# Making the sums of two of four chunk pairs for channel mixers 2 to 4 in the stage before each mixer

## The chip, the cores and the metric

The kernel runs on one core of one Trainium2 chip. Its engines work side by side, each on its own queue of instructions, in the order in which that queue was written: TensorE (PE in the profile: matmuls; PEld is its weight load), VectorE (DVE), ScalarE (ACT), GpSimd (POOL), and SyncE (SP), which here only issues DMAs. An instruction that waits holds up everything behind it on its engine. The metric is the device time of one execution in microseconds (us), the median of several runs.

## The reference

One sequence of 512 tokens of 1024 features goes through two layers. Each layer is a channel mixer, a token mixer and a second channel mixer, so there are four channel mixers; the token mixers are latent attention (MLA) in layer 1 and sparse attention (NSA) in layer 2.

```python
def rmsnorm(x, g):
    return x * rsqrt(mean(x * x, axis=-1) + 1e-6) * g

def swiglu(x, w_gate, w_up, w_down):          # 1024 -> 2816 -> 1024
    return (silu(x @ w_gate) * (x @ w_up)) @ w_down

for i in range(2):
    h = h + 0.5 * swiglu(rmsnorm(h, ffn_norm_a[i]), ...a[i])
    h = h + mixer_i(rmsnorm(h, mix_norm[i]))  # i = 0: MLA, i = 1: NSA
    h = h + 0.5 * swiglu(rmsnorm(h, ffn_norm_b[i]), ...b[i])
out = rmsnorm(h, final_norm)
```

Everything is float32.

## The kernel before

**Layout.** The residual `h` lies in SBUF transposed: eight chunks `h[0]` to `h[7]`, each 128 features by 512 tokens. A float32 operand is split into a high part (an ACT copy that rounds) and a low part (DVE: the value less the high part), and a product is three matmuls: high weight by high value, high weight by low value, low weight by high value. A chunk's weights can therefore not be multiplied through before DVE has made their low part, which the third matmul reads. Weights arrive by DMA in a raw tile (`wr`, two buffers) and are split into one of two tiles `w` that take turns (`slab_ahead`: ACT L176 the high part, DVE L178 the low part). A `w` tile is free for the next weights when the chunk two places earlier has been multiplied.

**A channel mixer** (`ffn`, called for 0 to 3; I call them mixers 1 to 4) has 22 blocks of 128 hidden units. The first three (`PLAIN`) are done by plain matmuls of `x = h * gain` (`plain`, L401 to L403); call their weight slabs g0, u0, g1, u1, g2, u2 in their order. Blocks 3 to 21 use a form of Strassen's scheme with seven products in place of eight (`wsums`, `product`): it pairs chunk p with chunk p + 4 (p = 0 to 3) and halves of the tokens, and needs for each pair four sums of quarters. `combine(p)` makes them: ACT scales both chunks into `y` (L267, twice), DVE forms four sums of quarters in `u` in three instructions (L271, 128x512; L272 and L273, 128x256 each), and `split` makes high and low part of `u` in a tile `four` (ACT L205 and DVE L206, 128x1024 each). In mixers 2 to 4 the four `combine` calls stand behind the plain blocks: pair 0 behind the first, pair 1 behind the second, pairs 2 and 3 behind the third. `four` has four buffers.

**The end of the stage ahead of a mixer** is where the residual's chunks end, one by one, in the order 0, 4, 1, 5, 2, 6, 3, 7 (`self.order`). Mixer 3 follows mixer 2: there each chunk takes 24 matmuls (L462 to L464) with its own 512-column weights. Mixers 2 and 4 follow attention: there each chunk takes 12 matmuls of 512 columns (`w_o1`, L197 to L199), and one 1024-column weight slab serves two chunks. When a chunk's matmuls end, DVE adds it to the residual (L468, in attention L708), and `norm_chunk` makes `x` of it (ACT L208, DVE L209) and its squares (ACT L285), which POOL sums up (L289).

**What sets the order.** The kernel is written against a layer that records all instructions with their dependences and then schedules each engine's queue by itself; what is written earlier goes first among what is ready in that layer's own reckoning. So a call that is moved in the source moves instructions on ACT and DVE past others, and the result is a fixed queue.

In the built program the chunks are named by a number: `h_101` is chunk 0, `h_102` chunk 1, and so on to `h_108`, chunk 7. The functions that the change touches, with the line numbers of the profile:

Of the kernel before, what the change touches and what calls it, by code (L numbers as in the profile page):

```python
# [11 lines left out]
F32 = mybir.dt.float32  # L12
# [6 lines left out]
P = 128  # L19
# [24 lines left out]
TURN = "mm", "S", "T", "mm", "S", "T", "T"  # L44
FGAINS = "a0", "b0", "a1", "b1"
LASTK = 4
HS = S // 2
KP = KC // 2
PLAIN = 3
PAD = 16  # L50
# [11 lines left out]
class Kern:  # L62
# [157 lines left out]
    def norm_chunk(self, c):  # L220
# [5 lines left out]
        else:  # L226
            self.sumsq(self.h[c], self.s2 is None)

    def norm_split(self, c):
        t = self.xp.tile([P, 2 * S], F32R, tag="x", bufs=KC, name="x")  # L230
        if self.to_ffn:

            g = self.ngains[:, self.nng + c : self.nng + c + 1]
            v = t.rearrange("p (e z n) -> p e z n", e=2, z=2)
            hi, lo, src = v[:, :, 0, :], v[:, :, 1, :], self.h[c].rearrange("p (e n) -> p e n", e=2)
            self.split(src, hi, lo, gain=g)
            for e in range(2):
                self.xc["LR"[e], c] = v[:, e, 0, :], v[:, e, 1, :]
        else:
            self.split(self.h[c], t[:, :S], t[:, S:], gain=self.gains[:, self.ng + c : self.ng + c + 1])  # L240
            self.xh.append(t[:, :S])
            self.xl.append(t[:, S:])
# [12 lines left out]
            return self.xp.tile([P, S], F32R, tag="w2", bufs=2, name="q")  # L255
        return self.qt[(self.nq - self.nq // 3 - 1) % 4]

    def combine(self, p):


        nc, fp = self.nc, self.fp
        y = fp.tile([P, 1024], F32, tag="fh", bufs=3, name="y")
        u = fp.tile([P, 1024 + 2 * PAD], F32, tag="fl", bufs=3, name="u")[:, :1024]
        for e in range(2):
            c = p + KP * e
            with self.tc.issue_after(self.weights.ins) if self.weights else nullcontext():
                nc.scalar.activation(y[:, e * S : e * S + S], self.h[c], AF.Copy, scale=self.gains[:, self.ng + c : self.ng + c + 1])  # L267
            self.weights = None
        q = lambda t, i: t[:, i * HS : i * HS + HS]
        two = lambda t: t.rearrange("p (a n) -> p a n", n=HS)  # L270
        nc.vector.tensor_tensor(two(u[:, :S]), q(y, 1)[:, None, :].to_broadcast([P, 2, HS]), two(y)[:, 0:4:3, :], op=ALU.subtract)  # L271
        nc.vector.tensor_tensor(q(u, 2), q(y, 0), q(u, 1), op=ALU.subtract)  # L272
        nc.vector.tensor_tensor(q(u, 3), q(y, 2), q(u, 2), op=ALU.subtract)  # L273
        t = self.four()
        self.split(u, t[:, :1024], t[:, 1024:])
        for i, j in enumerate((5, 7, 6, 4)):
            self.xc[j, p] = q(t, i), q(t, i + 4)
        for j, x in zip((1, 2, 3), (("L", p), ("L", p + KP), ("R", p + KP))):
            self.xc[j, p] = self.xc[x]
# [116 lines left out]
    def plain1(self, w, k, out):  # L396
        (wh, wl), mm = w, self.nc.tensor.matmul
        for e in range(2):
            (xh, xl), o = self.xc["LR"[e], k], out[:, e * HS : e * HS + HS]

# [26 lines left out]
    def ffn(self, idx, gain_next, ap, tp):  # L427
# [6 lines left out]
        def gate(f, g):  # L434

            t = tg[f] = tp.tile([P, S], F32, tag="tg", bufs=2, name="tg")
            nc.vector.tensor_tensor(t, g, row, op=ALU.mult)
            nc.scalar.activation(t, t, AF.Silu, scale=-1.0)
            nc.vector.tensor_tensor(t, t, row, op=ALU.mult)
# [17 lines left out]
        def down(p, w, b0, b1):  # L457
            for k in range(b0, b1):
                wh, wl = w[0][:, k - b0], w[1][:, k - b0]
                for x in range(0, S, HS):  # L460
                    o, xh, xl = p[:, x : x + HS], ah[k][:, x : x + HS], al[k][:, x : x + HS]
                    nc.tensor.matmul(o, wh, xh, start=k == b0 and x == 0, stop=False, skip_group_check=True)  # L462
# [20 lines left out]
        def tokens(t):  # L483

            xts.append(tp.tile([P, D], F32, tag="fr", bufs=3, name="xt"))
            with self.tc.issue_after(self.high.ins):
                nc.sync.dma_start(xts[t], a["x_tok"][t * P : (t + 1) * P, :])

        def squares(t):
            nc.scalar.activation(xts[t], xts[t], AF.Square, accum_out=sums[:, t : t + 1])  # L490

        def late():
            for c in self.late:
                self.sumsq(self.h[c])
            return self.norm_col(D, self.s2)
# [3 lines left out]
        for f, g in enumerate(gates):  # L499
            u = tu[f] = self.bank(("mm", "S")[f % 2], "pu")  # L500
            if idx == f == 0:
                self.first_block((g, u))
                self.third_slab(a["w_gu"][0, 1, 0])
                self.ahead.insert(0, self.wslab(a["w_gu"][0, 1, 1], (KC, P), "half"))
                for t in range(3):
                    tokens(t)
                squares(0)
                tokens(3)
                squares(1)
            else:  # L510
                self.plain(idx, f, 0, g)
            if f == 0 and idx > 1:
                col = late()
            if f == 1 and idx == 0:
                squares(2)
                squares(3)
                col = self.rsqrt_col(sums, D)
            if idx or f:
                self.plain(idx, f, 1, u)
            if f == 0 and idx == 1:  # L520

                col = late()
            if f == 1:
                nc.scalar.activation(self.tiny[:, 4:5], col[:, 0:1], AF.Silu, scale=-1.0)
                pb = self.norm_bcast(col)
                row = tp.tile([P, S], F32, tag="row", bufs=1, name="row")
                self.spread = nc.scalar.activation(row, pb, AF.Copy)
                for e in range(2):
                    gate(e, gates[e])
                    act(e)  # L530
            elif f:
                gate(f, g)
                act(f)
            for p in (((0,), (1,), (2, 3)) if idx else ((0, 1), (2,), (3,)))[f]:
                self.combine(p)
        t = self.tiny
        for i, g in enumerate(gates[::-1]):
# [32 lines left out]
        if gain_next == "fin":  # L570

            hs, out = [self.parts(self.four(F32)) for _ in range(4)], []
            for t in range(4):
                for b in range(2):
                    p = self.mm_bank("ph")
# [9 lines left out]
        for c in self.order:  # L585
            p = self.mm_bank("pd")
            down(p, self.wslab(a["w_down"][idx, c, :, tail * P :], (NF - tail, P), "act"), tail, NF)
            add(c, p)
            self.norm_chunk(c)
            if ahead and c == self.order[-1]:  # L590
                self.ahead.append(ahead())

    def last(self, src, ah, al, ap, ht, hs):
# [16 lines left out]

        ks = range(NF - LASTK, NF)
        ends = {k: slab(k) for k in ks}
# [91 lines left out]
    def w_o1(self, w, oh, ol, c, e, final):  # L704
        p = self.mm_bank("po")
        for k in range(4):
            self.mm3(p, w[0][:, e, k], w[1][:, e, k], oh[k], ol[k], k == 0, k == 3)
        self.nc.vector.tensor_tensor(self.h[c], p, self.h[c], op=ALU.add)  # L708
        if final:
            self.norm_chunk(c)  # L710

    def stats(self, n):

# [820 lines left out]
```

## Time and profile before

| | |
|---|---|
| Median of 3 runs | 1863.41 us (1863.02 to 1865.26) |
| The profiled execution | 1862.05 us |
| its span, first to last instruction | 1860.3 us |
| PE busy | 1845.7 us, 99% of the span, 14464 matmuls |
| DVE busy | 1507.4 us, 81% |
| ACT busy | 1064.5 us, 57% |
| POOL busy | 296.7 us, 16% |
| granted TensorE clock, mean | 0.999 |

The span is what the profiler saw between the program's first and last instruction; the execution's own time is longer by 1.75 us around it. A matmul is counted as busy from its start to its modelled end, and matmuls overlap, so that a PE wait of less than about 0.17 us does not show as idle time. In the chain of work that ended last, PE has 93% of the span.

### The profile page before, as it was taken

The numbers are of one execution on the slowest core, as the hardware profiler recorded it, in microseconds if no ns is written. First come the engines' busy times: TensorE is split into PE (matmuls) and PEld (weight loads), VectorE is DVE, ScalarE is ACT, GpSimd is POOL, SyncE is SP. The second block draws the span as 40 slices with busy tenths as digits, with TensorE's granted clock in tenths as the row PEclk, the third lists the DMA queues.
The fourth block names the chain that finished last, engine by engine and source line by source line (L and its number), as shares of the span: only waits on it lengthen the run. The fifth ranks groups of instructions, "written<-read, shape, count | busy, mean of one in ns | idle before, by whom it ended". The sixth has DMA issues, their size and how long they took to land.

```text
span 1860.3 us, 37031 instructions
## 1 busy us (share of the span) xinstructions
PE 1845.7 (99%) x14464; PEld 1763.4 (95%) x14464; DVE 1507.4 (81%) x2810; ACT 1064.5 (57%) x1997; POOL 296.7 (16%) x370
## 2 busy tenths in 40 slices
PE   9999999999999999999999999999999999999998
PEld 9999999888889999999999999988888889999997
DVE  8988886688779988886898888666878888888885
ACT  7555553567666555554655545446776865555554
POOL 0000000258830000001000000022666620000000
PEclk9999999999999999999999999999999999999999
DMA  6433331434433433322443332162433133433321
GB/s 238 132 108 103 103 92 48 117 105 103 114 123 112 119 103 109 110 73 72 138 118 110 109 106 81 45 183 82 108 108 103 40 118 116 121 104 107 103 78 69
DMA packets 84351, 196.64 MB, mean 106 GB/s; under 512 B 10944, under 2 KB 38464, under 8 KB 84176
## 3 DMA queue, kind: packets, MB, share of 16 engines
q1 hardware_dynamic: 81664, 191.34, 34.9%
q10 hardware_dynamic: 2512, 2.93, 0.5%
q8 instruction: 114, 1.87, 0.4%
q14 instruction: 61, 0.50, 0.1%
HBM read 178.44 MB, written 2.16 MB: 97 GB/s over the span
## 4 chain that ended last, share of the span: by engine, by line
PE 93%; DVE 3%; ACT 1%; issue 1%; POOL 1%; DMA 0%; ACTq 0%; POOLq 0%; DVEq 0%
PE pd L462 8%; PE pd L464 8%; PE pd L463 8%; PE px L386 6%; PE px L388 6%; PE px L387 5%; PE pg L386 4%; PE pg L388 4%; PE pg L387 4%; PE pq L386 4%; PE pq L388 4%; PE pq L387 4%; PE o L1337 2%; PE pt L1310 2%; PE po L197 2%; PE po L199 2%
## 5 line engine op out<-in xcount | busy, mean ns | idle before, releaser
L462 PE MATMUL pd<-ah,wd 128*128 128x256 f32 x1152 | 318.3, 276 | 0.0
L464 PE MATMUL pd<-ah,wd 128*128 128x256 f32 x1152 | 318.3, 276 | 0.0
L463 PE MATMUL pd<-al,wd 128*128 128x256 f32 x1152 | 318.3, 276 | 0.0
L289 POOL TENSOR_TENSOR s<-s,sq 128x512 f32<-128x512 f32 x38 | 54.7, 1441 | 1050.3 <-ACT sq L285 1050.3
L462 PEld LDWEIGHTS pd<-ah,wd 128*128 128x128 f32 x1152 | 216.3, 188 | 0.0
L464 PEld LDWEIGHTS pd<-ah,wd 128*128 128x128 f32 x1152 | 216.3, 188 | 0.0
L463 PEld LDWEIGHTS pd<-al,wd 128*128 128x128 f32 x1152 | 216.3, 188 | 0.0
L206 DVE TENSOR_TENSOR w<-wr,w 128x1024 fp32r<-128x1024 f32 x72 | 88.2, 1225 | 120.7 <-ACT w L205 120.4
L386 PE MATMUL px<-four,wh 128*128 128x256 f32 x608 | 168.4, 277 | 0.4 <-ACT wh L205 0.2
L388 PE MATMUL px<-four,wl 128*128 128x256 f32 x608 | 168.2, 277 | 0.2 <-DVE wl L206 0.2
L386 PE MATMUL pq<-four,wh 128*128 128x256 f32 x608 | 168.1, 276 | 0.2 <-ACT uq L556 0.2
L387 PE MATMUL px<-four,wh 128*128 128x256 f32 x608 | 168.0, 276 | 0.0
L388 PE MATMUL pq<-four,wl 128*128 128x256 f32 x608 | 167.9, 276 | 0.0
L387 PE MATMUL pq<-four,wh 128*128 128x256 f32 x608 | 167.9, 276 | 0.0
L468 DVE SCALAR_TENSOR_TENSOR h<-pd,h 128x512 f32<-128x512 f32 x216 | 148.3, 686 | 15.4 <-PE pd L464 15.2
L205 ACT ACTIVATE wd<-wdr 128x384 fp32r<-128x384 f32 x192 | 99.2, 519 | 103.8 <-issue 64.6
L176 ACT ACTIVATE w<-wr 128x1024 fp32r<-128x1024 f32 (+3 forms) x89 | 80.8, 908 | 87.5 <-PE pd L464 20.6
L206 DVE TENSOR_TENSOR wd<-wdr,wd 128x384 fp32r<-128x384 f32 x192 | 105.8, 553 | 20.1 <-ACT wd L205 20.0
L178 DVE TENSOR_TENSOR w<-wr,w 128x1024 fp32r<-128x1024 f32 (+3 forms) x75 | 78.3, 1044 | 50.0 <-ACT w L176 49.8
L728 ACT ACTIVATE p<-p,small 128x512 f32<-128x512 f32 (+2 forms) x192 | 106.9, 558 | 19.0 <-DVE small L727 15.3
L386 PEld LDWEIGHTS px<-four,wh 128*128 128x128 f32 x608 | 114.1, 188 | 1.0 <-ACT wh L205 0.4
L388 PEld LDWEIGHTS px<-four,wl 128*128 128x128 f32 x608 | 114.2, 188 | 0.6 <-DVE wl L206 0.6
(379 smaller groups left out, 6264.9 us busy)
## 6 DMA issues: line engine op xcount, KB each, us to landing
wr<-in_w_gu SPq DMA_DIRECT2D x93, 512.0 KB, 3.5
ru<-in_w_gu SPq DMA_DIRECT2D x76, 512.0 KB, 4.3
wdr<-in_w_down SPq DMA_DIRECT2D x192, 192.0 KB, 2.5
wr<-in_w_down SPq DMA_DIRECT2D x24, 256.0 KB, 2.6
wr<-in_mla_w_o SPq DMA_DIRECT2D x8, 512.0 KB, 3.4
th<-btab_d SPq DMA_DIRECT2D x16, 256.0 KB, 3.7
wr<-in_nsa_w_q SPq DMA_DIRECT2D x8, 512.0 KB, 3.8
wr<-in_nsa_w_o SPq DMA_DIRECT2D x8, 512.0 KB, 3.7
```

Source lines behind the costliest of these rows:

```text
L176: self.copied = nc.scalar.activation(wh[:, m], raw[:, m], AF.Copy)
L178: nc.vector.tensor_tensor(wl[:, m], raw[:, m], f32v(wh[:, m]), op=ALU.subtract)
L205: nc.scalar.activation(hi, src, AF.Copy)
L206: (nc.gpsimd if pool else nc.vector).tensor_tensor(lo, src, f32v(hi), op=ALU.subtract)
L386: mm(out, wh[:, p], xh, start=first and p == 0, stop=False, skip_group_check=True)
L387: mm(out, wh[:, p], xl, start=False, stop=False, skip_group_check=True)
L388: mm(out, wl[:, p], xh, start=False, stop=last and p == KP - 1, skip_group_check=True)
L462: nc.tensor.matmul(o, wh, xh, start=k == b0 and x == 0, stop=False, skip_group_check=True)
L463: nc.tensor.matmul(o, wh, xl, start=False, stop=False, skip_group_check=True)
L464: last = nc.tensor.matmul(o, wl, xh, start=False, stop=k == b1 - 1, skip_group_check=True)
L468: nc.vector.scalar_tensor_tensor(self.h[c], p, 0.5, self.h[c], op0=ALU.mult, op1=ALU.add)
L728: nc.scalar.activation(p_sb[:, :n], p_sb[:, :n], AF.Exp, bias=nm, scale=-1.0, accum_out=sm)
```

## The change

`combine` for pairs 0 and 1 (`EARLY`) is called in the stage before mixers 2, 3 and 4, right behind `norm_chunk` of chunk 4 and of chunk 5, the second chunk of each pair. It is not done ahead of mixer 1, whose input comes by DMA. Its scratch (`y` and `u`, 2048 columns in all) is then a buffer of `four` (`spare`), which both early pairs share, since the usual scratch belongs to the mixer's own pools. In the mixer, pair 2 is made behind the first plain block and pair 3 behind the second. The number of instructions of each kind stays as it was.

```diff
+EARLY = 0, 1
...
+    def combine_early(self, c):
+        if self.to_ffn and c - KP in EARLY:
+            if c == KP:
+                self.spare = self.four(F32)
+            self.combine(c - KP, self.spare)
...
-    def combine(self, p):
+    def combine(self, p, spare=None):
...
-        y = fp.tile([P, 1024], F32, tag="fh", bufs=3, name="y")
-        u = fp.tile([P, 1024 + 2 * PAD], F32, tag="fl", bufs=3, name="u")[:, :1024]
+        if spare is None:
+            y = fp.tile([P, 1024], F32, tag="fh", bufs=3, name="y")
+            u = fp.tile([P, 1024 + 2 * PAD], F32, tag="fl", bufs=3, name="u")[:, :1024]
+        else:
+            y, u = spare[:, :1024], spare[:, 1024:]
...
-            for p in (((0,), (1,), (2, 3)) if idx else ((0, 1), (2,), (3,)))[f]:
+            for p in (((2,), (3,), ()) if idx else ((0, 1), (2,), (3,)))[f]:
                 self.combine(p)
...
             add(c, p)
             self.norm_chunk(c)
+            self.combine_early(c)
...
         if final:
             self.norm_chunk(c)
+            self.combine_early(c)
```

In the changed file the lines behind the edits are numbered higher: L178 is L179 there, L206 is L207, L209 is L210, L267 is L277, L271 to L273 are L281 to L283, L285 is L295, L468 is L478, and L708 is L719.

**VectorE, end of mixer 2.** Before, the queue holds for each chunk its addition, the low part of the weights of the chunk two places later, and the low part of `x`. Row 1250 (`w<-wr,w`) makes the low part for chunk 6.

```order
1246 L468 SCALAR_TENSOR_TENSOR h_102<-pd,h_102 128x512
1247 L178 TENSOR_TENSOR w<-wr,w 128x512
1248 L209 SCALAR_TENSOR_TENSOR x<-h_102,ngains,x 128x2x256
1249 L468 SCALAR_TENSOR_TENSOR h_106<-pd,h_106 128x512
1250 L178 TENSOR_TENSOR w<-wr,w 128x512
1251 L209 SCALAR_TENSOR_TENSOR x<-h_106,ngains,x 128x2x256
1252 L468 SCALAR_TENSOR_TENSOR h_103<-pd,h_103 128x512
```

Now the same place reads as follows. `four<-four` at L281 to L283 and L207 are the early pairs: the first pair in rows 1245 to 1252, the second from row 1254.

```order
1246 L478 SCALAR_TENSOR_TENSOR h_102<-pd,h_102 128x512
1247 L282 TENSOR_TENSOR four<-four 128x256
1248 L179 TENSOR_TENSOR w<-wr,w 128x512
1249 L283 TENSOR_TENSOR four<-four 128x256
1250 L210 SCALAR_TENSOR_TENSOR x<-h_102,ngains,x 128x2x256
1251 L478 SCALAR_TENSOR_TENSOR h_106<-pd,h_106 128x512
1252 L207 TENSOR_TENSOR four<-four 128x1024
1253 L210 SCALAR_TENSOR_TENSOR x<-h_106,ngains,x 128x2x256
1254 L281 TENSOR_TENSOR four<-four 128x512
1255 L478 SCALAR_TENSOR_TENSOR h_103<-pd,h_103 128x512
1256 L282 TENSOR_TENSOR four<-four 128x256
1257 L179 TENSOR_TENSOR w<-wr,w 128x512
```

The low part of chunk 6's weights has moved from ahead of chunk 2's addition (`h_103`) to behind it, and behind two instructions of the second pair.

**ScalarE, the same place.** Before, each chunk's weights (`w<-wr`) come ahead of `x` and the squares; row 787 is chunk 6's high part.

```order
784 L176 ACTIVATE w<-wr 128x512
785 L208 ACTIVATE x<-h_102,ngains 128x2x256
786 L285 ACTIVATE sq<-h_102 128x512
787 L176 ACTIVATE w<-wr 128x512
788 L208 ACTIVATE x<-h_106,ngains 128x2x256
789 L285 ACTIVATE sq<-h_106 128x512
790 L176 ACTIVATE w<-wr 128x512
```

Now (row 786 is still chunk 2's high part; `four<-h` at L277 is the scaling, `four<-four` at L206 the high part of the sums):

```order
786 L177 ACTIVATE w<-wr 128x512
787 L209 ACTIVATE x<-h_102,ngains 128x2x256
788 L295 ACTIVATE sq<-h_102 128x512
789 L277 ACTIVATE four<-h_102,gains 128x512
790 L206 ACTIVATE four<-four 128x1024
791 L209 ACTIVATE x<-h_106,ngains 128x2x256
792 L295 ACTIVATE sq<-h_106 128x512
793 L277 ACTIVATE four<-h_106,gains 128x512
794 L177 ACTIVATE w<-wr 128x512 x2
```

The high part of chunk 6's weights now stands behind the first pair's high part, which waits for DVE, and behind all of chunk 5's work.

**VectorE, end of NSA (ahead of mixer 4).** Before, row 2287 (`w<-wr,w`) is the low part of slab g0, the first that mixer 4 multiplies:

```order
2283 L708 TENSOR_TENSOR h_103<-po,h_103 128x512
2284 L178 TENSOR_TENSOR w<-wr,w 128x1024
2285 L209 SCALAR_TENSOR_TENSOR x<-h_103,ngains,x 128x2x256
2286 L708 TENSOR_TENSOR h_107<-po,h_107 128x512
2287 L178 TENSOR_TENSOR w<-wr,w 128x1024
2288 L209 SCALAR_TENSOR_TENSOR x<-h_107,ngains,x 128x2x256
2289 L708 TENSOR_TENSOR h_104<-po,h_104 128x512
```

Now slab g0's low part is row 2297:

```order
2286 L719 TENSOR_TENSOR h_103<-po,h_103 128x512
2287 L179 TENSOR_TENSOR w<-wr,w 128x1024
2288 L207 TENSOR_TENSOR four<-four 128x1024
2289 L210 SCALAR_TENSOR_TENSOR x<-h_103,ngains,x 128x2x256
2290 L281 TENSOR_TENSOR four<-four 128x512
2291 L719 TENSOR_TENSOR h_107<-po,h_107 128x512
2292 L282 TENSOR_TENSOR four<-four 128x256
2293 L719 TENSOR_TENSOR h_104<-po,h_104 128x512
2294 L283 TENSOR_TENSOR four<-four 128x256
2295 L210 SCALAR_TENSOR_TENSOR x<-h_107,ngains,x 128x2x256
2296 L210 SCALAR_TENSOR_TENSOR x<-h_104,ngains,x 128x2x256
2297 L179 TENSOR_TENSOR w<-wr,w 128x1024
```

It has moved behind chunk 3's addition (`h_104`), which needs the end of chunk 3's matmuls, and behind the `x` of chunks 6 and 3.

## Rows read from the trace of the kernel before

**Rows 1.** The page's busy time, share and instructions of the engines.

```profile
PE 1845.7 (99%) x14464; PEld 1763.4 (95%) x14464; DVE 1507.4 (81%) x2810; ACT 1064.5 (57%) x1997; POOL 296.7 (16%) x370
```

**Rows 2.** Busy us by engine, summed over the first 60 us of mixers 2, 3, 4.

```profile
sum 180.00, PE 179.04 PEld 177.49 DVE 162.45 ACT 117.70 POOL 7.98; mean PE 59.68 PEld 59.16 DVE 54.15 ACT 39.23 POOL 2.66
```

**Rows 3.** Timeline of DVE, end of mixer 2: start, us, instruction, idle before.

```profile
870.49 0.69 DVE L468 SCALAR_TENSOR_TENSOR h<-pd,h 128x512 f32<-128x512 f32 x1 [0.48 <-PE pd L464]
871.16 0.69 DVE L178 TENSOR_TENSOR w<-wr,w 128x512 fp32r<-128x512 f32 x1
871.98 0.75 DVE L209 SCALAR_TENSOR_TENSOR x<-h,ngains,x 128x512 fp32r<-128x512 f32 x1
873.22 0.69 DVE L468 SCALAR_TENSOR_TENSOR h<-pd,h 128x512 f32<-128x512 f32 x1 [0.49 <-PE pd L464]
```

**Rows 4.** Timeline of PE there: the third matmul of chunk 6.

```profile
873.24 0.28 PE L464 MATMUL pd<-ah,w 128*128 128x256 f32 x1
```

**Rows 5.** Timeline of ACT, end of mixer 2.

```profile
867.82 0.64 ACT L176 ACTIVATE w<-wr 128x512 fp32r<-128x512 f32 x1 [0.80 <-PE pd L464]
868.50 0.73 ACT L208 ACTIVATE x<-h,ngains 128x512 fp32r<-128x512 f32 x1
869.13 0.62 ACT L285 ACTIVATE sq<-h 128x512 f32<-128x512 f32 x1
```

**Rows 6.** Groups of DVE and ACT: count | busy us, mean ns | idle before.

```profile
L206 DVE TENSOR_TENSOR four<-u,four 128x1024 fp32r<-128x1024 f32 x16 | 19.5, 1222 | 1.5 <-ACT four L205 1.5
L271 DVE TENSOR_TENSOR u<-y 128x512 f32<-128x512 f32 x16 | 10.9, 685 | 0.0
L273 DVE TENSOR_TENSOR u<-y,u 128x256 f32<-128x256 f32 x16 | 6.7, 422 | 0.1
L267 ACT ACTIVATE y<-h,gains 128x512 f32<-128x512 f32 x32 | 20.8, 708 | 0.0
L205 ACT ACTIVATE four<-u 128x1024 fp32r<-128x1024 f32 x16 | 16.8, 1057 | 7.8 <-DVE u L273 7.8
```

**Rows 7.** Timeline of DVE, end of NSA.

```profile
1507.51 1.78 DVE L209 SCALAR_TENSOR_TENSOR x<-h,ngains,x 128x512 fp32r<-128x512 f32 x1
1509.82 1.21 DVE L178 TENSOR_TENSOR w<-wr,w 128x1024 fp32r<-128x1024 f32 x1
1510.95 0.74 DVE L209 SCALAR_TENSOR_TENSOR x<-h,ngains,x 128x512 fp32r<-128x512 f32 x1
1511.61 0.68 DVE L708 TENSOR_TENSOR h<-po,h 128x512 f32<-128x512 f32 x1
```

**Rows 8.** Timeline of POOL, the same place.

```profile
1507.37 1.38 POOL L289 TENSOR_TENSOR s<-s,sq 128x512 f32<-128x512 f32 x1 [0.86 <-ACT sq L285]
```

**Rows 9.** Busy us by engine, 1497 to 1511 us, the end of NSA.

```profile
1497.00:1511.00 14.00, 14.00 (x62) 11.39 (x61) 12.94 (x15) 10.04 (x15) 5.86 (x4) 1.00 0.25 77
```

**Rows 10.** Timeline of PE: mixer 4's third matmul, of slab g0.

```profile
1513.42 0.28 PE L403 MATMUL pg<-x,w 128*128 128x256 f32 x1
```

**Rows 11.** Timeline of DVE, end of MLA: low part of chunks 3 and 7's weights.

```profile
536.22 1.22 DVE L178 TENSOR_TENSOR w<-wr,w 128x1024 fp32r<-128x1024 f32 x1 [0.45 <-ACT w L176]
```

**Rows 12.** Timeline of PE: third matmul of MLA's chunk 3.

```profile
540.77 0.39 PE L199 MATMUL po<-oh,w 128*128 128x512 f32 x1
```

**Rows 13.** Timeline of DVE: slab u2's low part in mixers 2 and 4.

```profile
569.93 1.23 DVE L178 TENSOR_TENSOR w<-wr,w 128x1024 fp32r<-128x1024 f32 x1 [1.28 <-ACT w L176]
...
1537.58 1.23 DVE L178 TENSOR_TENSOR w<-wr,w 128x1024 fp32r<-128x1024 f32 x1 [2.05 <-ACT w L176]
```

**Rows 14.** Page: DMA issues of a chunk's weights, KB, us to landing.

```profile
wr<-in_w_down SPq DMA_DIRECT2D x24, 256.0 KB, 2.6
```

**Rows 15.** Busy us by engine at the end; PEclk ahead of the last two numbers.

```profile
1853.50:1856.20 2.70, 0.00 (x0) 0.00 (x0) 1.91 (x7) 1.46 (x4) 0.00 (x0) 1.00 0.00 0
1856.20:1860.30 4.10, 0.00 (x0) 0.00 (x0) 0.10 (x1) 0.07 (x1) 0.00 (x0) 0.51 0.33 128
```

**Rows 16.** Timeline of PE at the start: ten matmuls of 512 columns.

```profile
1.05 4.63 PE L95 MATMUL warm<-ones 128*128 128x512 f32 x10 [1.05 <-DVE ones L92]
```

## Prediction

> **What bounds the kernel now.** I read the page first: PE is busy for 1845.7 us [rows 1] of a span of 1860.3. So the change, which adds no matmul and takes none away, can only act through PE's waits, in two places: the first tens of us of mixers 2 to 4, from which two of four `combine` calls leave, and the ends of the stages ahead, into which they go. The table by stage gives the first place: in the first 60 us of the three mixers together, PE idles for 180 - 179.04 = 0.96 us [rows 2]. A wait under 0.17 us does not show there, so I allow as much again: about 2 us is all that relief at the mixers' starts can give back.
>
> For the second place I read the timelines. At the end of mixer 2 PE does not idle. The additions of two chunks are 873.22 - 870.49 = 2.73 us apart [rows 3], which is PE's own time for a chunk. DVE keeps that pace because three instructions of 0.69, 0.69 and 0.75 us fit into it, with some 0.5 us of idle time left. What PE waits for next is a weight's low part: chunk 6's is done at 871.16 + 0.69 = 871.85 [rows 3], and chunk 6's third matmul reads it at 873.24 [rows 4], 1.4 us later. So the slack is 1.4 us, and what is put ahead of that instruction decides.
>
> **What a pair costs.** On DVE one instruction of 685 ns, two of 422 (the second shape, L272, is like L273) and one of 1222: 2.75 us. On ACT two of 708 and one of 1057 ns: 2.47 us [rows 6]. In each of three stages two pairs are moved, so 5.5 us of DVE and 4.9 us of ACT; nothing is added over the whole kernel. Instructions that follow each other start some 0.08 us ahead of the listed end of the one before (1509.82 + 1.21 against 1510.95 [rows 7]); I take that off. `combine` issues no DMA.
>
> **End of mixer 2.** The new order puts the low part of chunk 6's weights behind chunk 2's addition. That addition cannot start before chunk 2's matmuls end, 873.22 [rows 3]. Behind it come a 128x256 sum and the low part: 873.22 + 0.69 + 0.42 + 0.69 - 0.16 = 874.9. PE wants it at 873.24, so it waits 1.6 us whatever else happens. That is the lower bound.
>
> DVE will not be ready at 873.22, though, since the sums hang on ACT. Chunk 4's ACT work stands one period ahead of the rows shown for chunk 1: its squares start at 869.13 - 2.73 = 866.4 [rows 5], its scaling ends at 867.7. Then, each step behind the one before:
> - DVE: first sum of pair 0 to 868.4, chunk 1's addition to 869.0.
> - ACT: chunk 1's x, squares and scaling (0.73 + 0.62 + 0.71) to 870.9, pair 0's high part to 871.9, chunk 5's three to 873.8.
> - DVE: first sum of pair 1 to 874.5, chunk 2's addition to 875.1, second sum to 875.4, chunk 6's low part to 876.1.
>
> That is 2.9 us later than PE wants it. POOL makes it worse. In NSA's end an x low part took 1.78 us in place of 0.74 while POOL summed squares at 1507.37 for 1.38 us [rows 7, 8]: it stood until POOL had ended, 1.04 us. Two such sums fall into the walk above, for 2.9 + 2.0 = 4.9 us. At mixer 2's end they now fall into gaps of DVE, and the early pairs fill those gaps. I take the middle, **3.9 us**, bounds 1.6 and 4.9.
>
> The Trainium skill (SBUF — State Buffer, section "Who interferes with whom") says that a VectorE instruction with two SBUF inputs and a GpSimd instruction that reads SBUF lock each other out for a whole instruction, and that the order of issue decides who waits. The trace agrees (the 1.78 us). By that rule alone the term would be 4.9, without it 2.9.
>
> **End of NSA.** Slab g0's low part ended at 1509.82 + 1.21 = 1511.03 [rows 7] and is read at 1513.42 [rows 10]. Now there stand ahead of it: pair 0 (2.75 - 0.3), three sums of pair 1 (1.53 - 0.24), and, which followed it before, x of chunk 6, chunk 3's addition and its x (0.66 + 0.60 + 0.66). Together 5.7 us. DVE idled for 14 - 12.94 = 1.06 us in the 14 us up to then [rows 9]; if all of that is used up, g0's low part ends at 1515.7, 2.2 us late. From below: chunk 3's matmuls end one chunk before g0's first; 12 matmuls of 512 columns are as many columns as 24 of 256, so 2.73 us, at about 1510.5. Addition, one sum, two x and the low part behind it (0.68 + 0.42 + 1.48 + 1.21 - 0.32) end at 1514.0: 0.5 us late. From above: two more collisions with POOL, 4.2. The collisions of before are in the 1511.03 already; I take **2.8 us**. Chunk 7's x now stands behind three scalings on ACT (2.1 us later), but it is read last of g0, which itself starts 2.8 us later; without that cover it would cost up to 2.1 in place of the 2.8.
>
> **End of MLA.** The low part for chunks 3 and 7 ended at 536.22 + 1.22 = 537.44 [rows 11] and is read at 540.77 [rows 12]: 3.3 us of slack. Ahead of it come pair 0 (2.45), chunk 2's addition and chunk 5's x (1.3), less the 0.45 us that DVE idled before it: 540.7, just in time. One or two collisions would make 1 to 2 us. Bounds 0 and 2.0; I take **0.3**.
>
> **The mixers' starts.** DVE gets rid of 5.5 us in the first 15 us. But by slab u2 DVE had caught up even before: it idled 1.28 us in mixer 2 and 2.05 us in mixer 4, waiting for ACT [rows 13]. What comes after that does not know of the early pairs. Bounds 0 and 2.0 us of gain; I take **0.4**.
>
> **Costed at nothing.** The scratch tile needs a `four` buffer whose readers are matmuls of the stage ahead; PE runs in order, so they are over when chunk 0 is multiplied. If they were not, the first scaling would wait and every step above with it. Chunk 7's raw weights load into the buffer that chunk 6's low part frees: 876.1 to 878.1, and 2.6 us to landing [rows 14], so 878.7 to 880.7. They are split when chunk 6's matmuls end, which is 873.0 + 2.7 and the lateness of 2.9 to 4.9: 878.6 to 880.6. This just fits; whatever the load is longer comes on top.
>
> **Sum.** 3.9 + 2.8 + 0.3 - 0.4 = 6.6 us. The profiled execution took 1862.05 us, so 1868.7 by its measure; the median of the runs shown is 1863.41, 1.36 higher, and against that I predict 1870.0 us. I call a change of under 0.2%, 3.7 us, no change, about what a measurement of this kernel can tell.
>
> **Rivals.**
> - *The stalls stay at their floor.* POOL keeps out of DVE's way, and the additions come as soon as the matmuls end: 1.6 + 0.5 + 0 less 0.4 to 2.0 gives 1863.5 to 1865.1, say 1864.6. For it: ACT and DVE had idle time (57% and 81% over the span). Against: the walk needs only the queue's order and durations that hardly vary.
> - *The TensorE clock drops during the long wait.* At the end of this trace PE has no matmul from 1853.5 on, and the granted clock, 1.00 until then and for 2.7 us more, is 0.51 in what follows, the lower of its two levels (1.2 GHz) [rows 15]. At the start ten matmuls of 512 columns took 4.63 us, 0.46 each [rows 16], twice the 2.73 / 12 = 0.23 of later ones. If the wait at mixer 2's end is as long as 4.9 us, the matmuls behind it might run at half speed for about as long as at the start, 5 us: 2.5 us more, or 5 if NSA's does the same, so 1872.5 to 1875. Against: two matmuls of chunk 6 stand in the middle of the wait. The Trainium skill (TensorE: Matmul & The Clock Gate, Part 1) has the same rule, that the full clock is given for activity and taken back without it.
> - *Relief wins, and it is not slower.* It turns on chunk 6's low part being ready by 873.24 and g0's by 1513.42. Then only the mixers' starts count, and the time is down by up to 2.0 us: 1861.4. For it: DVE is busy for 162 of those 180 us [rows 2]. Against: the addition of chunk 2 alone comes too late.
>
> **How the numbers follow.** My forecast 0.60, its own range 1867.2 to 1873.5 (3 to 4 us either way, from the bounds of the two large terms); the floor 0.22; the clock 0.12; relief 0.06. Slower by over 0.2%, that is above 1867.1: 0.60 + 0.12 less a little, 0.71. Within 0.2%: the floor and most of relief, 0.27. Faster by more would need nearly twice what PE's waits at the mixers' starts hold: 0.02. The range takes in the floor but for its lower end, and the clock but for its upper: 1864.0 to 1874.5, and leaves out some 0.19.
>
> **What would show it.** In the new profile PE should wait at the end of mixer 2, in the sixth of eight chunks, for DVE `w` (the low part) for 3 us or more after a shorter wait for ACT `w`; at mixer 4's first slab for DVE `w` again, for 2 to 3 us; at MLA's end hardly at all. DVE should have no idle time between chunk 4's and chunk 7's additions, and slab u2's low part should find DVE idle as before. I am wrong if PE's starts keep their distance of 2.73 us per chunk there, if the waits are there but given back within the mixer, or if the clock falls.

## The result and the profile after

The changed kernel takes 1879.0 us (median of 5 runs, 1877.7 to 1882.3), the kernel before 1864.1 (5 runs on the same chip). The ratio is 1.0084, 95% interval 1.0072 to 1.0095: 14.9 us slower. I had forecast 1870.0, at most 1874.5. The sign was right, and the size was less than half of what came.

The page of the changed kernel (profiled execution 1881.35 us, span 1879.6), the line that answers to [rows 1]:

```profile
PE 1854.0 (99%) x14464; PEld 1769.3 (94%) x14464; DVE 1513.5 (81%) x2810; ACT 1064.4 (57%) x1997; POOL 300.9 (16%) x370
```

With the same number of matmuls PE is busy for 8.3 us more. So part of the loss is not waiting: some matmuls ran slower. What PE waited for (instruction and what released it: us in total, times, longest):

```profile
PE pg L413 <- DVE w L179: 3.8, 1, 3.8
PE po L200 <- DVE w L179: 2.9, 2, 1.6
PE pd L474 <- DVE w L179: 1.9, 1, 1.9
PE pd L472 <- ACT w L177: 1.3, 1, 1.3
PE pg L412 <- DVE x L210: 0.7, 1, 0.7
```

These five are not in the kernel before: 10.6 us. The two of `pd` are at mixer 2's end; those of `po` are one at MLA's end (1.6) and one at NSA's (1.3); `pg` for `w` is mixer 4's slab g0, and `pg` for `x` is mixer 2's slab g0. Behind mixer 2's end and behind mixer 4's g0 the matmuls were slow. Busy time in those two stretches (us and count of PE, PEld, DVE, ACT, POOL, then the granted clock, DMA share, GB/s):

```profile
884.30:887.80 3.50, 3.50 (x19) 3.50 (x18) 2.31 (x4) 1.04 (x2) 2.33 (x1) 0.51 0.62 202
1529.40:1536.30 6.90, 6.12 (x28) 6.12 (x29) 6.90 (x9) 2.75 (x5) 1.52 (x1) 0.51 0.76 255
```

The clock is at the lower of its two levels (1.2 GHz) there, so half of PE's 9.6 us, 4.8, is lost. Waits and clock make 15.4 us of the span's 19.3. The other 3.9 lie in small pieces that I did not place, 1.1 of them ahead of the first early pair. The profiled execution of after is 2.3 us above its median and that of before 2.0 below its own, which makes 19.3 out of 14.9.

Nothing came back inside the mixers that can be put down to the change: the matmuls of mixer 4's slab u2 and the last ones of mixer 4 start 19.39 and 19.40 us later than before. In mixers 2 and 3 the lateness dips by 0.3 to 0.5 us and rises again, as it also does in a run without early pairs (the one with the sums on DVE).

Mixer 2's end on DVE, from chunk 1's addition on (start, us, instruction, idle before and its releaser); in the kernel before [rows 3] this was addition, low part and `x`, with idle time behind them:

```profile
874.07 0.68 DVE L478 SCALAR_TENSOR_TENSOR h<-pd,h 128x512 f32<-128x512 f32 x1
...
876.61 0.68 DVE L478 SCALAR_TENSOR_TENSOR h<-pd,h 128x512 f32<-128x512 f32 x1
877.63 1.31 DVE L207 TENSOR_TENSOR four<-four 128x1024 fp32r<-128x1024 f32 x1 [0.34 <-ACT four L206]
878.86 1.75 DVE L210 SCALAR_TENSOR_TENSOR x<-h,ngains,x 128x512 fp32r<-128x512 f32 x1
880.54 0.68 DVE L281 TENSOR_TENSOR four<-four 128x512 f32<-128x512 f32 x1
881.14 0.68 DVE L478 SCALAR_TENSOR_TENSOR h<-pd,h 128x512 f32<-128x512 f32 x1
881.74 0.41 DVE L282 TENSOR_TENSOR four<-four 128x256 f32<-128x256 f32 x1
882.08 0.68 DVE L179 TENSOR_TENSOR w<-wr,w 128x512 fp32r<-128x512 f32 x1
```

And PE there, the first matmuls of chunk 6:

```profile
878.32 0.28 PE L474 MATMUL pd<-ah,w 128*128 128x256 f32 x1
879.91 0.39 PE L472 MATMUL pd<-ah,w 128*128 128x256 f32 x1 [1.31 <-ACT w L177]
...
880.66 0.28 PE L473 MATMUL pd<-al,w 128*128 128x256 f32 x1
882.81 0.38 PE L474 MATMUL pd<-ah,w 128*128 128x256 f32 x1 [1.87 <-DVE w L179]
```

This is the predicted queue and the predicted chunk: a first sum, chunk 2's addition, a second sum, and only then chunk 6's low part. Chunk 2's matmuls were over at 878.6, but DVE came to its addition at 881.14. Ahead of it stood the first pair's low part, which had waited for ACT, `x` of the chunk before, which took 1.75 us in place of 0.74, and the second pair's first sum.

NSA's end, DVE, up to g0's low part (the row of 2.29 us; the changed kernel's answer to [rows 7]):

```profile
1513.55 0.69 DVE L719 TENSOR_TENSOR h<-po,h 128x512 f32<-128x512 f32 x1 [0.38 <-PE po L200]
1514.16 0.68 DVE L281 TENSOR_TENSOR four<-four 128x512 f32<-128x512 f32 x1
1514.76 1.85 DVE L210 SCALAR_TENSOR_TENSOR x<-h,ngains,x 128x512 fp32r<-128x512 f32 x1
1516.53 1.52 DVE L282 TENSOR_TENSOR four<-four 128x256 f32<-128x256 f32 x1
...
1525.47 2.44 DVE L210 SCALAR_TENSOR_TENSOR x<-h,ngains,x 128x512 fp32r<-128x512 f32 x2
1527.84 2.29 DVE L179 TENSOR_TENSOR w<-wr,w 128x1024 fp32r<-128x1024 f32 x1
```

POOL at the same place:

```profile
1514.76 3.00 POOL L299 TENSOR_TENSOR s<-s,sq 128x512 f32<-128x512 f32 x2 [1.03 <-ACT sq L295]
...
1527.59 1.46 POOL L299 TENSOR_TENSOR s<-s,sq 128x512 f32<-128x512 f32 x1 [0.89 <-ACT sq L295]
```

From 1513.55 to 1530 DVE has no idle time at all. An `x` that takes 0.74 us elsewhere takes 1.85, a sum of 0.41 takes 1.52, and the low part of 1.21 takes 2.29, each while POOL sums squares. PE reads that low part at 1530.18.

MLA's end: DVE's low part for chunks 3 and 7, POOL, and PE's third matmul of chunk 3 [rows 11, 12]:

```profile
541.52 2.30 DVE L179 TENSOR_TENSOR w<-wr,w 128x1024 fp32r<-128x1024 f32 x1
541.26 1.47 POOL L299 TENSOR_TENSOR s<-s,sq 128x512 f32<-128x512 f32 x1 [3.60 <-ACT sq L295]
543.87 0.50 PE L200 MATMUL po<-oh,w 128*128 128x512 f32 x1 [1.58 <-DVE w L179]
```

### The profile page after: what moved, and what is told of

The parts are those of the page before. It is cut to its first block, busy times and chain, and to the rows that moved or that the text cites. A ratio compares the mean times of both kernels' runs of the same rounds, so it can differ in the third digit from the quotient of the medians.

```text
span 1879.6 us, 37041 instructions
## 1 busy us (share of the span) xinstructions
PE 1854.0 (99%) x14464; PEld 1769.3 (94%) x14464; DVE 1513.5 (81%) x2810; ACT 1064.4 (57%) x1997; POOL 300.9 (16%) x370
## 4 chain that ended last, share of the span: by engine, by line
PE 91%; DVE 5%; ACT 2%; issue 1%; POOL 1%; DMA 0%; ACTq 0%; POOLq 0%; DVEq 0%
PE pd L474 8%; PE pd L472 8%; PE pd L473 8%; PE px L396 5%; PE px L398 5%; PE px L397 5%; PE pg L396 4%; PE pg L397 4%; PE pg L398 4%; PE pq L396 4%; PE pq L397 4%; PE pq L398 4%; PE o L1349 2%; PE pt L1322 2%; PE pp L200 1%
## 5 line engine op out<-in xcount | busy, mean ns | idle before, releaser
L299 POOL TENSOR_TENSOR s<-s,sq 128x512 f32<-128x512 f32 x38 | 59.2, 1557 | 1062.3 <-ACT sq L295 1062.2
L207 DVE TENSOR_TENSOR w<-wr,w 128x1024 fp32r<-128x1024 f32 x72 | 88.2, 1225 | 123.2 <-ACT w L206 122.9
L478 DVE SCALAR_TENSOR_TENSOR h<-pd,h 128x512 f32<-128x512 f32 x216 | 147.8, 684 | 15.2 <-PE pd L474 15.0
L206 ACT ACTIVATE wd<-wdr 128x384 fp32r<-128x384 f32 x192 | 99.2, 518 | 102.3 <-issue 65.6
L179 DVE TENSOR_TENSOR w<-wr,w 128x1024 fp32r<-128x1024 f32 (+3 forms) x75 | 79.4, 1059 | 62.1 <-ACT w L177 61.8
L207 DVE TENSOR_TENSOR wd<-wdr,wd 128x384 fp32r<-128x384 f32 x192 | 105.5, 551 | 18.8 <-ACT wd L206 18.3
L740 ACT ACTIVATE p<-p,small 128x512 f32<-128x512 f32 (+2 forms) x192 | 106.9, 558 | 19.1 <-DVE small L739 15.4
```

The costliest lines, as they stand in the source:

```text
L179: nc.vector.tensor_tensor(wl[:, m], raw[:, m], f32v(wh[:, m]), op=ALU.subtract)
L206: nc.scalar.activation(hi, src, AF.Copy)
L207: (nc.gpsimd if pool else nc.vector).tensor_tensor(lo, src, f32v(hi), op=ALU.subtract)
L478: nc.vector.scalar_tensor_tensor(self.h[c], p, 0.5, self.h[c], op0=ALU.mult, op1=ALU.add)
L740: nc.scalar.activation(p_sb[:, :n], p_sb[:, :n], AF.Exp, bias=nm, scale=-1.0, accum_out=sm)
```

## The experiments

All were timed beside the kernel before on the same chip, and differences are to its median in that group (1862.9 to 1864.2). Line numbers shift by a few from kernel to kernel.

### One stage at a time

Three kernels: the pairs are made early ahead of one mixer only, and the other two mixers make them as before.

```diff
-EARLY = 0, 1
+EARLY = {"b0": (0, 1)}        # mixer 2; "a1" mixer 3; "b1" mixer 4
...
-        if self.to_ffn and c - KP in EARLY:
+        if self.to_ffn and c - KP in self.early:      # EARLY.get(gain, ())
```

> Only mixer 2's first two pairs are made early, at the end of MLA. In the changed kernel's trace PE waits 1.75 us there for the low part of chunks 3 and 7's weights and 0.9 us for the last chunk's x. Theory (low parts queued behind the early pairs on DVE and ACT): about 3 us over the kernel before, 1866 to 1868, granted clock 1.00 throughout, since no wait is over 2 us. Rival (the falls of the clock are the main part): 1864 to 1865.5, no difference that can be told. Rival (the whole loss needs several stages, each pushing the next): also near 1864.

> Only mixer 3's first two pairs are made early, at the end of mixer 2. Theory: PE waits about 1.5 us for the high part and 2.0 us for the low part of chunk 6's weights, as in the changed kernel, so 3.5 us, and the clock falls to half for some 3.4 us behind it, which costs 1.7 us: 1868.5 to 1870. Rival (clock is the main part): half or more of the loss lies in slices with a granted clock under 1; if the clock does not fall here alone, 1865. Rival (load of DVE and ACT, not their order): the waits are spread over chunks 2 to 7 rather than in chunk 6.

> Only mixer 4's first two pairs are made early, at the end of NSA. Theory: PE waits 1.5 us in chunks 3 and 7 and 3.9 us for slab g0's low part, and the clock falls to half for up to 6.8 us (3.4 us lost): 1870 to 1873. The three kernels with one stage each should add up to the changed kernel: excesses of about 3, 5 and 7 to 8 us against 14.9. Rival (stages push each other): the sum of the three excesses is well under 14.9, under 11.

Measured: 1866.66 us (ratio 1.0015, 1.0006 to 1.0024), 1870.09 (1.0033, 1.0020 to 1.0045) and 1871.30 (1.0040, 1.0027 to 1.0053). That is 2.5, 5.9 and 7.1 us more, within 0.1 us of the theory's ranges, together 15.5 against 14.9. So the stages lose each by itself and do not push each other. The mixer 3 kernel waits for the same two things for as long as the changed kernel:

```profile
PE pd L475 <- DVE w L180: 1.9, 1, 1.9
PE pd L473 <- ACT w L178: 1.3, 1, 1.3
```

Its clock falls behind them, and so it does behind the waits of the other two (mixer 4's kernel: 3.8 us for g0's low part):

```profile
879.40:883.80 4.40, 4.37 (x24) 4.37 (x25) 3.80 (x4) 1.37 (x2) 1.72 (x1) 0.61 0.37 82
```

```profile
1521.20:1527.20 6.00, 5.95 (x28) 5.95 (x29) 6.00 (x8) 2.02 (x4) 1.52 (x1) 0.52 0.82 272
```

By the granted clock that is 4.37 x 0.39 = 1.7 and 5.95 x 0.48 = 2.9 us lost. The expected "granted clock 1.00 throughout" in the mixer 2 kernel was wrong: it waited 2.4 us at MLA's end and had a granted clock of 0.50 for the 3.0 us behind it.

### Weights first

The split of the weights two chunks ahead is written right behind a chunk's matmuls and ahead of its addition; `w_o` in the same way, with slabs g0 and u0 of the next mixer as its last two.

```diff
...
-            down(p, self.wslab(a["w_down"][idx, c, :, tail * P :], (NF - tail, P), "act"), tail, NF)
+            down(p, ws[i], tail, NF)
+            ws += [slab(x) for x in self.order[i + 2 : i + 3]]
             add(c, p)
             self.norm_chunk(c)
             self.combine_early(c)
...
```

> All early pairs stay as in the changed kernel, but the high and low parts of the next chunk's weights (and, at the ends of MLA and NSA, of slabs g0 and u0) are put into ACT's and DVE's queues ahead of the addition, x and sums of the chunk before. Theory (the order in the queues): the three waits go, 1863 to 1866.5, no fall of the clock. Rival (sheer load of DVE and ACT at the stage ends): the lateness only moves to x and the sums, 1872 or more. Rival (collisions of DVE with POOL's square sums are the main part): some half comes back, 1868 to 1873.

Measured 1883.89 us (1.0104, 1.0089 to 1.0120): slower still. My first theory, that the order in the queue alone makes the loss, fell here. The low part of g0 is waited for less, 1.6 us, and other operands more:

```profile
PE pg L412 <- DVE x L210: 4.7, 4, 2.3
PE pg L411 <- ACT x L209: 3.0, 3, 2.0
PE pd L474 <- DVE w L179: 2.3, 2, 1.4
```

The same order without early pairs:

> The kernel before with the same order of the weights' parts as in the run with the weights ahead, and no early pairs. Control: if that order by itself costs or gives nothing, 1862 to 1866, and the 20 us of that run are due to the early pairs. If the order by itself is bad (x of the last chunks late), 1868 or more with PE waiting for x at the first slab.

Measured 1868.47 us (1.0029, 1.0017 to 1.0040), 5.1 more. So this order costs 5 by itself, and the early pairs add 1883.89 - 1864.17 - 5.1 = 14.6 to it, in total as much as in the other order. Between these two orders other operands are late, and the sum of what is lost is the same; stage by stage it is not (table further down).

### Half the pairs

`EARLY = (0,)` in all three stages; the second pair goes back into the mixer.

> Only the first of the two pairs is made early, in all three stages; the second is made in the mixer's first slab, as in the kernel before. The run with the weights ahead (slower than the changed kernel, with PE waiting for x instead) has put a second theory beside the first: the early pairs are more DVE and ACT work than these stage ends have room for, and the order only settles what is late. Theory (room): half the work takes far less than half of 14.9 us, since it first fills the idle time: 1864 to 1868, no fall of the clock. Rival (order alone): about half or more, 1870 to 1874, since add, sums and x still stand ahead of the low parts.

Measured 1874.26 us (1.0056, 1.0042 to 1.0070), 10.9 more: half the work and over two thirds of the loss. The expected "far less than half" was wrong. With POOL summing, the first pair alone is already too much: the longest wait is for the low part at mixer 2's end.

```profile
PE pd L475 <- DVE w L180: 2.6, 1, 2.6
```

### Without POOL's sums

```diff
-        else:
-            self.sumsq(self.h[c], self.s2 is None)
+        elif not self.to_ffn or self.s2 is None:
+            self.sumsq(self.h[c], self.s2 is None)
+        else:
+            self.nc.scalar.activation(self.scratch("sq"), self.h[c], AF.Square)
```

> The changed kernel without POOL's sums of the squares in the mixers' norms at the stage ends (left out: the squares of all but the first chunk are made and not added, so the scale of the norm is another). In the changed kernel's trace DVE instructions at the three stage ends take 12.8 us longer than the usual time of their kind, against 6.8 in the kernel before, while POOL sums. Rival (collisions are the main part): 1864 to 1868, most of the 14.9 us gone. Theory (order and room): at most half is gone, 1871 to 1877; mixer 2's end, where only 1.7 us of the 12.8 lie, keeps its waits of 1.5 and 2.0 us.

> The kernel before with the same sums left out, as a control. Both theories: 1862 to 1864, since PE hardly waits at the stage ends of that kernel.

Measured 1867.75 us with early pairs (1.0022, 1.0013 to 1.0031) and 1862.76 without (0.9997, 0.9988 to 1.0006). So without POOL's sums the early pairs cost 5.0 us (the two runs against each other), in place of 14.9. What is left of PE's waits at the three ends:

```profile
PE pd L474 <- ACT w L177: 0.9, 1, 0.9
PE pd L476 <- DVE w L179: 0.8, 1, 0.8
...
PE pg L415 <- DVE w L179: 0.6, 1, 0.6
```

The clock falls behind the first two. Its granted mean over the 6 us from there on is 0.72, which is 5.16 x 0.28 = 1.4 us lost:

```profile
875.00:881.00 6.00, 5.16 (x26) 4.74 (x27) 4.54 (x8) 2.84 (x5) 0.00 (x0) 0.72 0.39 115
```

With the waits' 2.3 us that is 3.7 of the 5.0; I did not place the remaining 1.3.

The weights-first order without the sums:

> The run with the weights ahead (1883.9), and POOL's sums of the squares at the stage ends left out as in the two runs before (left out: the sums, so the norm's scale is another). The runs so far: the sums left out takes the changed kernel from 15 us over to 5, so POOL's collisions with DVE are about two thirds, and the order of the weights alone did not help. Theory now (collisions fill the room that DVE had left; what is left, 5 us, is the order at mixer 2's end, 1.1 and 0.9 us of waits and the fall of the clock behind them): with both away 1862 to 1865. Rival (sheer load of two pairs, with or without POOL): 1867 or more, waits for x.

Measured 1867.07 us (1.0021, 1.0012 to 1.0030), 4.1 more, with 1.5 us of waiting for `x` at mixer 2's start. The time and the wait are the rival's. But this order cost 5.1 us without any early pair, and no run has it without both the pairs and the sums, so it is not shown that the two pairs' load is what is left.

### More sums, and a scratch tile for each pair

```diff
             nc.gpsimd.tensor_tensor(self.s2, self.s2, sq, op=ALU.add)
+            if self.to_ffn:
+                nc.gpsimd.tensor_tensor(sq[:, :HS], self.s2[:, :HS], sq[:, :HS], op=ALU.add)
```

> The kernel before, with half as much again of POOL's sums at the stage ends (behind each sum of 512 columns another of 256, whose result nobody reads). No early pairs. Theory (collisions cost only where DVE has no room for them): 1863 to 1866. Rival (collisions cost by themselves, early pairs or not): the 10 us that the sums cost in the changed kernel come to 3 to 5 here, 1867 to 1869.

Measured 1872.12 us (1.0054, 1.0041 to 1.0067), 9.2 more without any early pair, outside both expectations. But the run does not separate what it should: the longer sums also hold the buffer of the squares, and ACT, which waits 0.2 us for POOL there in the kernel before, waits 10.7.

```profile
ACT sq L296 <- POOL sq L302: 10.7, 8, 1.7
```

The changed kernel with `self.combine(c - KP, self.four(F32))` in place of the shared scratch:

> The changed kernel with a scratch tile of its own for each of the two early pairs. In the changed kernel's trace ACT's scaling for pair 1 waits for DVE's sums of pair 0, which read the shared tile, 1.4 us in all three stages together, and x, squares and the weights' high parts stand behind it. Theory: this wait is a small part, 1877 to 1880. Rival (the shared tile is what ties ACT to DVE and makes both late): 1873 or less.

Measured 1879.67 us (1.0093, 1.0079 to 1.0107). The shared tile is no cause.

### The sums on DVE

```diff
-            nc.gpsimd.tensor_tensor(self.s2, self.s2, sq, op=ALU.add)
+            (nc.vector if self.to_ffn else nc.gpsimd).tensor_tensor(self.s2, self.s2, sq, op=ALU.add)
```

> The changed kernel with the seven sums of the squares of each of mixers 2 to 4 on DVE in place of POOL: no overlap of the two engines at the stage ends any more, but some 4.3 us more work on DVE per stage (7 of 0.69 us less the overlap), about as much as the 12.8 us by which DVE's instructions were stretched in the three stages together. Room theory (what counts is DVE's time at the stage end, stretched or worked): about the changed kernel, 1875 to 1882. Collision theory (it is the stretching at the wrong instruction that costs): nearer to the run without the sums, 1867 to 1872.

> The kernel before with the same sums on DVE, no early pairs. DVE trades 6.8 us of stretching in the three stages for some 13 us of work. Room theory: 1865 to 1870 (more POOL sums, which added as much, cost 9 us). Collision theory: 1862 to 1864, as fast as without the sums, and if the stretching did cost before, a little faster than the kernel before.

Measured 1883.00 us with early pairs (1.0105, 1.0091 to 1.0118) and 1862.45 without (0.9998, 0.9989 to 1.0007). No overlap with POOL is left, and the loss is there all the same, 20.1 us. The page of that kernel has DVE as busy as the changed kernel's, 1513.5:

```profile
PE 1851.6 (99%) x14464; PEld 1767.5 (94%) x14464; DVE 1512.3 (81%) x2831; ACT 1065.2 (57%) x1997; POOL 266.9 (14%) x349
```

This fits that DVE's time counts, whether POOL stretches it or DVE works the sums itself. The kernel before has some: in 20 us near the end of MLA, mixer 2 and NSA its DVE is idle for 5.5, 5.7 and 4.2 us,

```profile
526.00:546.00 20.00, 20.00 (x90) 16.37 (x89) 14.53 (x20) 11.57 (x17) 7.90 (x5) 1.00 0.40 125
859.00:879.00 20.00, 20.00 (x179) 20.00 (x178) 14.30 (x21) 11.58 (x20) 6.41 (x5) 1.00 0.31 85
1493.20:1513.20 20.00, 20.00 (x88) 15.89 (x87) 15.82 (x20) 12.17 (x18) 7.38 (x5) 1.00 0.29 85
```

which takes in the sums (7 of some 0.6 us), and nearly the pairs (5.5 us), but not both, and not the pairs and what POOL adds. This count is too wide, though: by it the first pair alone (2.75 us) would have fitted, and it cost 10.9. Most of that idle time lies ahead of chunk 4's addition, when there is nothing to sum yet, or behind the low part that was late. From chunk 4's addition to the end of that low part DVE is idle for 7.80 - 6.64 = 1.2, 1.2 and 0.8 us (MLA, mixer 2, NSA):

```profile
529.64:537.44 7.80, 7.80 (x36) 6.44 (x35) 6.64 (x9) 6.58 (x10) 3.01 (x2) 1.00 0.23 71
865.05:871.85 6.80, 6.80 (x62) 6.80 (x61) 5.63 (x8) 5.03 (x9) 2.70 (x2) 1.00 0.42 117
1497.82:1511.03 13.21, 13.21 (x59) 10.75 (x58) 12.37 (x15) 9.92 (x15) 5.86 (x4) 1.00 0.26 80
```

One caution: in the run with early pairs and sums on DVE the order of PE's matmuls at NSA's end moved as well, and 6.0 us of its waits are there, so 20.1 is not all DVE's.

Where each kernel loses can be read from PE alone: the table has by how much its lateness against the kernel before grows across each stage end, in us. It compares the start of the same matmul in both traces, at 528 and 583 us of the kernel before (MLA's end), 862 and 900 (mixer 2's), 1497 and 1552 (NSA's). Each row is one profiled execution.

| | MLA's end | mixer 2's end | NSA's end |
|---|---|---|---|
| the changed kernel | 3.1 | 6.0 | 8.1 |
| pair 0 alone | 4.2 | 4.4 | 2.6 |
| no sums | 0.1 | 3.9 | 1.1 |
| sums on DVE | 4.9 | 3.8 | 8.6 |
| weights first | 7.6 | 5.5 | 8.1 |
| weights first, no early pairs | 1.3 | 0.0 | 4.4 |
| weights first, no sums | 1.5 | 1.1 | 0.9 |

So the sums decide at the ends of MLA and NSA, where the early pairs cost 1.1 us or less without them. At mixer 2's end most of the loss stays without the sums, and there the other order helps: 1.1 in place of 3.9.

### Waits of a set length

The kernel before, with the low part of the sixth chunk's weights written several times over at the ends of mixers 1 to 3.

```diff
...
-                if not self.lo_pool:
+                for _ in range(0 if self.lo_pool else 1 + again):   # again = 4, 6, 9
                     nc.vector.tensor_tensor(wl[:, m], raw[:, m], f32v(wh[:, m]), op=ALU.subtract)
```

> The kernel before, with the low part of the sixth chunk's weights made again 4, 6 and 9 times over at the ends of mixers 1, 2 and 3, so that PE waits there for a set time and for nothing else. By the rows (0.69 us each, 1.4 us of slack) PE should wait about 1.2, 2.6 and 4.6 us. Theory (a wait of some 2 us or more takes half the clock away for some us, as behind the waits of 2.0 to 3.9 us in the runs so far): no fall behind the shortest, falls of 3 to 5.5 us behind the others, each worth 1.2 to 2.7 us; in all 1863.5 + 8.4 + 4 = 1876. Rival (the falls have to do with the early pairs or with POOL, not with the wait): no fall, 1872.

Measured 1889.36 us (1.0140, 1.0126 to 1.0154), 26.4 more. The repeats mixed with the other work, so the waits are not those expected: the first long one is 2.38 us in all three mixers, with others behind it in the second and third. All of PE's waits for these weights come to 12.6 us; I did not place the rest of the 26.4. The run still serves, with the same wait three times, behind the same 0.49 us for ACT. PE in mixers 1 and 2:

```profile
337.56 0.38 PE L474 MATMUL pd<-ah,w 128*128 128x256 f32 x1 [0.49 <-ACT w L179]
340.45 0.56 PE L476 MATMUL pd<-ah,w 128*128 128x256 f32 x1 [2.38 <-DVE w L181]
...
881.82 0.38 PE L474 MATMUL pd<-ah,w 128*128 128x256 f32 x1 [0.49 <-ACT w L179]
884.69 0.39 PE L476 MATMUL pd<-ah,w 128*128 128x256 f32 x1 [2.38 <-DVE w L181]
```

and the granted clock behind both, and behind that of mixer 3:

```profile
340.40:344.00 3.60, 3.55 (x17) 3.55 (x18) 2.34 (x2) 0.07 (x1) 1.64 (x1) 0.53 0.30 88
884.60:888.20 3.60, 2.86 (x22) 2.66 (x22) 3.53 (x5) 0.72 (x2) 1.66 (x1) 1.00 0.27 73
1226.80:1230.80 4.00, 3.94 (x22) 3.82 (x22) 3.90 (x6) 0.08 (x1) 1.66 (x1) 0.65 0.23 66
```

It fell in the first and the third and not in the second. So it needs no early pair, and the wait's length alone does not decide it.

## Why the prediction was wrong

- **What bounds the kernel; the place and the kind of loss.** Right: PE alone, the three stage ends, a low part behind chunk 2's addition, no gain at the mixers' starts. I took 0.4 us of relief, and none is seen.
- **End of mixer 2, 3.9 us.** Right in mechanism and near in size: 1.3 and 1.9 us in chunk 6, for ACT and DVE `w`, so 3.2, though the wait for DVE alone was to be 3 or more. The walk without POOL gave 2.9, and the run without the sums has 0.9 and 0.8, near the lower bound of 1.6; the sums add 1.5 where I took up to 2.0. DVE was not without idle time up to chunk 7's addition: it had caught up by chunk 6's and waited 1.17 us for PE.
- **End of NSA, 2.8 us.** Too small: 3.8 for g0's low part and 1.3 for the low part of chunks 3 and 7, for which I had no term. The floor of 0.5 holds without the sums (0.6). My step "The collisions of before are in the 1511.03 already; I take 2.8 us" failed: from chunk 5's addition on DVE had no gap left, and `x`, a sum of the pair and g0's low part were stretched by 1.1 us each while POOL summed.
- **End of MLA, 0.3 us.** The same error: 1.6 and 0.7 us. I had written that one or two collisions would make 1 to 2 us and set them aside; the low part there took 2.30 us, not 1.22, beside a sum of POOL's.
- **The clock, a rival at 0.12.** The forecast's sum had it at nothing, and I had named its fall as a sign of being wrong. It came along with the forecast rather than in its place: 1.7 and 3.1 us in the profiled execution. That "two matmuls of chunk 6 stand in the middle of the wait" kept nothing off: four stood there, and it fell.
- **Costed at nothing.** The scratch tile had a wait that I had not seen (pair 1's scaling behind pair 0's sums, 1.4 us at NSA's end); with a tile for each pair the time is no shorter. For chunk 7's weights PE does not wait in the new trace.

By terms: 6.6, and 2.0 more at MLA's end, 2.3 at NSA's, 0.4 for the relief, 4.8 for the clock, 0.7 less at mixer 2's: 15.4, the sum of waits and clock above. So the mechanism was right, and what failed are the collisions with POOL at MLA's and NSA's ends, which were set aside, and the clock, which was left out of the sum.

The cause, as far as the runs show it: between chunk 4's addition and the low part that PE reads next, DVE has some 1 us of idle time, and one pair takes 2.75. What does not fit must come out of the slack, which was 3.3 us at MLA's end, 2.4 at NSA's and 1.4 at mixer 2's. Without the sums of squares it nearly does at the first two, and the early pairs cost 5.0 us, most of it at mixer 2's end. With the sums, on POOL or on DVE, the next operands are late, for 15 to 20 us. The sums' share of some 10 us is shown by leaving them out; that the idle time and the slack set the rest is worked out from the rows and not shown by a run (at MLA's end pair 0 alone would have fitted by it and lost 4.2 us, with `x` of mixer 2's slab g0 late). The Trainium skill (SBUF — State Buffer, section "Who interferes with whom") has a VectorE instruction with two SBUF inputs contend with a GpSimd instruction that reads SBUF. The stretched rows agree (2.29 us in place of 1.21), but the run with the sums on DVE shows that this contention is not what the loss needs. How ACT's lateness shares in it was not tried apart, nor how much of mixer 2's end is the queue's order.

## What to carry to other kernels

Before work is moved into a stage, count the idle time of the engine that does it between the moment its input is there and the operand that will stand behind it, not over the stage's last 20 us; add the slack of that operand, and subtract what an engine that works at the same time stretches. If the work does not fit, price the lateness with the stretched durations and not with the means. When a new order only moves the lateness to other operands, look at each stage by itself: here the order helped at one end, without the sums, and not at the others. In this kernel waits of PE of 1 to 4 us cost up to another 3 us in clock behind them, and some cost nothing.

## What I had not expected of the hardware

The granted clock fell to about half (0.50 to 0.53) for 3 to 7 us behind single waits of 2.4 to 3.8 us, in kernels where it is 1.00 nearly everywhere else, and behind three waits of 2.38 us it was 0.53, 1.00 and 0.65. The Trainium skill (TensorE: Matmul & The Clock Gate, Part 1) has the full clock released by activity and throttled without it. The falls agree in that they came behind waits; what told the three apart stays open.
